# The mixer's two attentions as one pipeline of head pairs, with projections between its steps

## The chip, the cores and the metric

The kernel runs on one core of a Trainium2 chip. The metric is the device time of one execution in microseconds, as the median of three runs. The engines in the tables are TensorE (PE, with its weight loads as PEld), VectorE (DVE), ScalarE (ACT), GpSimd (POOL) and SyncE (SP, which issues the DMAs).

## The reference, cut to what matters

Two transformer blocks on 256 tokens of 1024 features. The first has two layers, each with a mixer between its feed-forward parts:

```python
(qa, ckv, iq, ik, iw, qs, ks, vs, cb, cc, ch, ga, gb, gc) = split(x @ w_in)
ckv = rms_norm(ckv, kv_g)
y_a = dsa_branch(qa, ckv, iq, ik, iw, w_uk, w_uv, rel_bias)   # 8 heads
y_b = stick_breaking_branch(qs, ks, vs)                       # 8 heads
y_c = short_conv_branch(cb, cc, ch, conv_w)
merged = (sigmoid(ga + b_gate[0]) * (y_a @ w_branch[0])
          + sigmoid(gb + b_gate[1]) * (y_b @ w_branch[1])
          + sigmoid(gc + b_gate[2]) * (y_c @ w_branch[2]))
return merged @ w_out
```

`dsa_branch` scores all earlier tokens with eight index heads (relu of dot products, weighted and added up), keeps the 64 best of each query, and then runs a softmax attention of eight heads over these, in a latent space of 128 columns that all heads share, with a bias by distance; `w_uv` takes each head's latent output to 64 columns. `stick_breaking_branch` weighs each earlier token by sigmoid(z) times the product of 1 - sigmoid(z) of the tokens between: a reverse cumulative product per row.

## The kernel before

Activations lie feature-major, [128 features, 256 tokens] a tile. Every projection is exact in float32: each operand is kept as a high and a low part, and one product is three matmuls (`mm3`, L241 to L243: high by high, high by low, low by high). Weights come in pieces of 512 KB by SP's DMA queue (`wf`), ScalarE casts the high part (`wh`, L236), VectorE subtracts it for the low part (`wl`, L237). `pair` projects two column tiles of 128 into one PSUM bank: 2 x 8 x 3 = 48 matmuls of 256 columns. PSUM has four banks with the tag `pa` (attention and transposes) and four with `pj` (projections). The pools of scratch tiles are fixed: eight of 512 columns (`a2`), four of 256 (`a1`).

The order of each engine's instructions is set by a scheduler: it takes the program as it is traced, with the tracing order as priority, and lets later instructions that are ready go ahead of earlier ones that would wait. So projections that are traced after an attention are found between its steps.

The mixer of one layer (`mixer`, L527) is traced so: values of the stick-breaking; latent and index projections; index scores, one head after the other, each in a bank of its own (L587, L588), added up on VectorE; the top-k on VectorE, 8 rounds for either half of the queries (L597, L598), and the mask `sel` (L600, L601); the attention's queries (2 pairs). Then a first pipeline of eight heads with four stages, each a head behind the one before (`skew`): `logits` (queries to latent space L626, copied by L627; bias plus mask on GpSimd L630, L631; logits L633, L634; VectorE adds the bias, L635; softmax L496 to L501 and L506), `turned` (three 128x128 transposes, L316, copied by L766), `latent` (L771, L772, copied by L649 into an `a1` tile) and `values` (L656: 64 columns of output; two heads share a bank, which is split into high and low part when the second is in). Then the queries and keys of the stick-breaking (4 pairs) and a second pipeline of eight heads with three stages: `sticks` (scores L675, L676; mask L678; two sigmoids L680, L682; the scan L687, L689), `turned`, and `broken` (L771, L772 with 64 columns of output). Then the convolution's four column tiles, 72 matmuls each, with six VectorE operations on each (L721 to L726 and the split); then 12 gate pairs, and eight output projections of the three branches (36 matmuls each) between them.

A filler runs beside all this: the second block's shifts and scales (`adaln`, L894), 4 matmuls of 32 columns a unit (L924), each unit with a weight of 512 KB (`wa`). `fill(place)` traces as many units as a table has for that visit of a place; logits and sticks have three each. `until` traces whatever is still missing when the second block needs it.

## Time and profile before

| | |
|---|---|
| median of three runs | 2645.27 us (2642.64 to 2647.34) |
| span of the profiled execution | 2638.9 us |
| TensorE busy | 2581.5 us, 98% |
| VectorE busy | 1495.0 us, 57% |
| ScalarE busy | 1176.3 us, 45% |
| stretch of the index scores and both attentions, layer 0 | 267.30 to 372.40 us |
| the same, layer 1 | 1019.90 to 1123.60 us |

Matmuls overlap in the array, so the busy time of one (0.28 us for 256 columns) is longer than the distance from its start to the start of the next; distances between starts tell what an instruction costs. "Idle before" names the engine and line that ended an idle time. The granted clock (PEclk) is a share of the full 2.4 GHz.

### The profile page before, as it was taken

How to read it: one execution, taken by the hardware profiler on the slowest of the kernel's cores; microseconds unless marked ns; L12 is line 12 of the kernel's file. 1: busy time of each engine (PE TensorE's matmuls, PEld its weight loads, DVE VectorE, ACT ScalarE, POOL GpSimd, SP SyncE). 2: the span in 40 equal slices, each digit the busy share in tenths (PEclk: the TensorE clock that was granted, in tenths of full speed). 3: DMA queues.
4: the chain of work that ended last, by engine and by line, in shares of the span. 5: the costliest groups of instructions: out<-in, count | busy, mean ns of one | idle time of the engine just before them, and what ended most of it. 6: DMA issues, size and time to landing. Idle time of an engine off the chain costs nothing.

```text
span 2638.9 us, 40347 instructions
## 1 busy us (share of the span) xinstructions
PE 2581.5 (98%) x15946; PEld 2178.1 (83%) x15946; DVE 1495.0 (57%) x3006; ACT 1176.3 (45%) x1953; POOL 43.2 (2%) x52
## 2 busy tenths in 40 slices
PE   8999999999999999999999999999999999999999
PEld 7997789969979978799699776567888776777997
DVE  5546765665456557655664757656222337555554
ACT  5444454554444444544544545444222325444443
POOL 0000100000000001000000000000000000010000
PEclk9999999999999999999999999899999999999999
DMA  7565335655556555256565542424222435432453
GB/s 256 189 216 191 133 112 181 200 204 206 189 179 208 197 173 204 90 168 205 203 223 191 184 152 80 140 102 150 104 96 96 161 106 186 121 72 64 169 192 136
DMA packets 136493, 424.19 MB, mean 161 GB/s; under 512 B 29752, under 2 KB 32480, under 8 KB 136304
## 3 DMA queue, kind: packets, MB, share of 16 engines
q1 hardware_dynamic: 136304, 421.62, 47.2%
q8 instruction: 125, 2.05, 0.3%
q14 instruction: 64, 0.52, 0.1%
HBM read 417.33 MB, written 4.24 MB: 160 GB/s over the span
## 4 chain that ended last, share of the span: by engine, by line
PE 87%; DVE 5%; DMA 4%; ACT 2%; issue 1%; SPq 0%; POOL 0%; ACTq 0%; DVEq 0%; POOLq 0%
PE pj L241 17%; PE pj L242 17%; PE pj L243 17%; PE pa L242 7%; PE pa L241 7%; PE pa L243 7%; PE pa L316 3%; PE pj L924 2%; DMA wf<-in_ffn_w_inA_dram 2%; PE pa L1392 1%; DVE wl L237 1%; DMA wa<-in_mod_wB_dram 1%; PE pj L1369 1%; DMA wf<-in_mix_A_dram 1%; PE pj L1276 1%
## 5 line engine op out<-in xcount | busy, mean ns | idle before, releaser
L237 DVE TENSOR_TENSOR wl<-wf,wh 128x1024 fp32r<-128x1024 f32 (+1 forms) x652 | 785.1, 1205 | 740.2 <-ACT wh L236 735.6
L236 ACT CAST wh<-wf 128x1024 fp32r<-128x1024 f32 (+1 forms) x652 | 670.6, 1032 | 929.9 <-PE pj L242 425.9
L241 PE MATMUL pj<-k,wh 128*128 128x256 f32 (+2 forms) x2896 | 841.7, 291 | 2.1 <-ACT k L236 2.1
L242 PE MATMUL pj<-k,wh 128*128 128x256 f32 (+2 forms) x2896 | 839.9, 290 | 0.0
L243 PE MATMUL pj<-k,wl 128*128 128x256 f32 (+2 forms) x2896 | 839.8, 290 | 0.0
L241 PEld LDWEIGHTS pj<-k,wh 128*128 128x128 f32 (+1 forms) x2896 | 555.3, 192 | 17.3 <-issue 7.0
L243 PEld LDWEIGHTS pj<-k,wl 128*128 128x128 f32 (+1 forms) x2896 | 555.0, 192 | 10.7 <-issue 3.4
L242 PEld LDWEIGHTS pj<-k,wh 128*128 128x128 f32 (+1 forms) x2896 | 555.0, 192 | 10.5 <-issue 3.2
L242 PE MATMUL pa<-wl,k 128*128 128x512 f32 x688 | 274.0, 398 | 0.0
L241 PE MATMUL pa<-wh,k 128*128 128x512 f32 x688 | 272.0, 395 | 0.0
L241 PE MATMUL pj<-wh,k 128*128 128x512 f32 (+1 forms) x616 | 247.8, 404 | 12.2 <-ACT wh L236 7.0
L242 PE MATMUL pj<-wl,k 128*128 128x512 f32 (+1 forms) x616 | 247.3, 402 | 0.0
L243 PE MATMUL pa<-wh,a 128*128 128x512 f32 x560 | 218.1, 389 | 0.0
L243 PE MATMUL pj<-wh,k 128*128 128x512 f32 (+1 forms) x496 | 198.5, 401 | 0.2 <-DVE k L237 0.2
L241 PEld LDWEIGHTS pj<-wh,k 128*128 128x128 f32 x616 | 117.4, 191 | 49.2 <-issue 8.3
L241 PEld LDWEIGHTS pa<-wh,k 128*128 128x128 f32 x688 | 128.8, 187 | 33.5 <-issue 0.8
L242 PEld LDWEIGHTS pa<-wl,k 128*128 128x128 f32 x688 | 129.2, 188 | 28.6 <-issue 1.0
L242 PEld LDWEIGHTS pj<-wl,k 128*128 128x128 f32 x616 | 117.3, 190 | 29.8 <-DVE wl L237 2.3
L236 ACT CAST k<-k 128x512 fp32r<-128x512 f32 (+2 forms) x152 | 85.7, 578 | 106.3 <-PE pa L242 39.0
L243 PEld LDWEIGHTS pa<-wh,a 128*128 128x128 f32 x560 | 105.3, 188 | 25.5 <-issue 0.4
L243 PEld LDWEIGHTS pj<-wh,k 128*128 128x128 f32 x496 | 94.9, 191 | 23.5 <-DVE jc L326 2.1
L237 DVE TENSOR_TENSOR a<-k,k 128x512 fp32r<-128x512 f32 x85 | 57.8, 687 | 50.4 <-ACT k L236 50.4
(252 smaller groups left out, 2523.4 us busy)
## 6 DMA issues: line engine op xcount, KB each, us to landing
wf<-in_ffn_w_inA_dram SPq DMA_DIRECT2D x262, 512.0 KB, 3.7
wf<-in_ffn_w_outB_dram SPq DMA_DIRECT2D x132, 512.0 KB, 3.8
wf<-in_mix_A_dram SPq DMA_DIRECT2D x108, 512.0 KB, 3.7
wa<-in_mod_wB_dram SPq DMA_DIRECT2D x96, 512.0 KB, 4.2
wf<-in_w_branchA_dram SPq DMA_DIRECT2D x32, 384.0 KB, 3.2
wf<-in_od_w_dram SPq DMA_DIRECT2D x24, 512.0 KB, 4.7
wf<-in_w_mix_outB_dram SPq DMA_DIRECT2D x16, 512.0 KB, 3.9
wf<-in_w_outB_dram SPq DMA_DIRECT2D x16, 512.0 KB, 7.9
```

The costliest lines, as they stand in the source:

```text
L236: self.nc.scalar.copy(h, x)
L237: self.nc.vector.tensor_tensor(l, x, h.bitcast(F32), ALU.subtract)
L241: mm(ps, sh, mh, start=start, stop=False)
L242: mm(ps, sh, ml, start=False, stop=False)
L243: mm(ps, sl, mh, start=False, stop=stop)
L316: self.nc.tensor.transpose(ps[:, i * P:(i + 1) * P], b, self.ident)
L924: mm(ps[32 * c:32 * c + 32, :256], self.cond[:, k], w[:, c * 256:c * 256 + 256], start=k == 0, stop=k == KT - 1)
L1276: mm(ps[:, j * T:(j + 1) * T], q["dqT"][b, h, c], k["dkT"][b, h], start=True, stop=True)
L1369: mm(ps[:, j * T:(j + 1) * T], q["qT"][hp // 4][b, hp % 4, c], k["kT"][hp // 4][b, hp % 4], start=True, stop=True)
L1392: mm(po[hp][b, c], kv[n // 2]["v"][n % 2][:, h * 64:h * 64 + 64], pT[:, n * P:(n + 1) * P], start=n == 0, stop=n == 3)
```

## The change

Index scores, stick-breaking scores and queries are computed by pairs of heads: a new function issues the matmuls of the two heads alternately, each head on its half of the array's rows and in its own bank. All six pairs of projections (queries of the attention, queries and keys of the stick-breaking) are traced ahead of the pipeline. There is one pipeline: eight units, the four head pairs of the attention and then the four of the stick-breaking, with five stages (`queries`, `weights`, `turned`, `values`, `heads`). After the second stage of each step a hook runs: a convolution tile in the steps 0 to 3, nothing in step 4, one gate pair in each step from 5 on. The latents of a pair share a bank and are copied at once (512 columns, an `a2` tile); the outputs of a pair are issued next to each other, on the two column halves of one bank. The calls of the filler at logits and sticks are gone.

```diff
-    def skew(self, units, *stages):
+    def skew(self, units, *stages, step=None):
...
             for n, stage in enumerate(stages):
                 if 0 <= t - n < len(units):
                     vals[t - n] = stage(*units[t - n], vals[t - n])
+                if n == 1 and step:
+                    step(t)
...
-        for h in range(8):
-            b = slice(64 * (h % 2), 64 * (h % 2) + 64)
-            ps = self.ps()
-            mm(ps[:, 0:P], iqT[b, h // 2, 0:P], ikT[b, 0:P], start=True, stop=True)
-            mm(ps[:, P:384], iqT[b, h // 2, P:T], ikT[b, :], start=True, stop=True)
...
+        for hp in range(4):
+            banks = self.causal_scores(iqT[:, hp], ikT)
...
-        def logits(h, _):
-            hp, i = divmod(h, 2)
-            if i == 0:
-                qls[hp] = self.a2().rearrange("p (c t) -> p c t", c=2)
-                for j in range(2):
-                    b = slice(64 * j, 64 * j + 64)
-                    ps = self.ps()
-                    mm(ps[:, :T], wuk[b, hp], qaT[b, hp], start=True, stop=True)
-                    A.mul(qls[hp][:, j], ps[:, :T], 0.125)
...
-            self.fill(f"logits{l}")
...
-        def latent(h, pT):
-            ps = self.ps()
-            self.causal_pv(ps[:, :T], [ckN[:, 0], ckN[:, 1]], pT)
-            ol = self.a1()
-            A.copy(ol, ps[:, :T])
-            return ol
-        def values(h, ol):
-            hp, i = divmod(h, 2)
-            if i == 0:
-                pos[hp] = self.ps()
-            mm(pos[hp][64 * i:64 * i + 64, :T], wuv[:, h], ol, start=True, stop=True)
-            if i == 1:
-                self.split(ys[0].h(hp), ys[0].l(hp), pos[hp][:, :T])
-        self.skew([(h,) for h in range(8)], logits, turned, latent, values)
...
-        def sticks(h, _):
-            hp, i = divmod(h, 2)
-            b = slice(64 * i, 64 * i + 64)
-            ps = self.ps()
-            mm(ps[:, 0:P], qsT[b, hp, 0:P], ksT[b, hp, 0:P], start=True, stop=True)
-            mm(ps[:, P:384], qsT[b, hp, P:T], ksT[b, hp], start=True, stop=True)
...
-            self.fill(f"sticks{l}")
...
-        def broken(h, pT):
-            hp, i = divmod(h, 2)
-            if i == 0:
-                pos[hp] = self.ps()
-            self.causal_pv(pos[hp][64 * i:64 * i + 64, :T], [vs[:, tb, h * 64:h * 64 + 64] for tb in range(NT)], pT)
-            if i == 1:
-                self.split(ys[1].h(hp), ys[1].l(hp), pos[hp][:, :T])
-        self.skew([(h,) for h in range(8)], sticks, turned, broken)
...
-        for t in range(4):
+        def conv(t):
...
+        def gate():
+            ps = self.pair(wA[15 + len(gates) // 2], xs)
...
+        def queries(kind, hp, _):
+            if kind:
+                return None
+            ql = self.a2().rearrange("p (c t) -> p c t", c=2)
+            banks = [self.ps() for _ in range(2)]
+            for j in range(2):
+                b = slice(64 * j, 64 * j + 64)
+                mm(banks[j][:, :T], wuk[b, hp], qaT[b, hp], start=True, stop=True)
+            for j in range(2):
+                A.mul(ql[:, j], banks[j][:, :T], 0.125)
+            return ql
+        def weights(kind, hp, ql):
+            if kind:
+                banks = self.causal_scores(qsT[:, hp], ksT[:, hp])
+                return [sticks(ps) for ps in banks]
+            out = []
...
+        def turned(kind, hp, ps):
+            return [self.causalT(p) for p in ps]
+        def values(kind, hp, pTs):
+            ps = self.ps()
+            if kind:
+                if hp == 0:
+                    ys[1] = Split(self, 4)
+                v = [[vs[:, tb, h * 64:h * 64 + 64] for tb in range(NT)] for h in (2 * hp, 2 * hp + 1)]
+                self.causal_pv([ps[64 * i:64 * i + 64, :T] for i in range(2)], v, pTs)
+                self.split(ys[1].h(hp), ys[1].l(hp), ps[:, :T])
+                return None
+            for i in range(2):
+                self.causal_pv([ps[:, i * T:(i + 1) * T]], [[ckN[:, 0], ckN[:, 1]]], pTs[i:i + 1])
+            ol = self.a2().rearrange("p (c t) -> p c t", c=2)
+            A.copy(ol, ps.rearrange("p (c t) -> p c t", c=2))
+            return ol
+        def heads(kind, hp, ol):
+            if kind:
+                return
+            ps = self.ps()
+            for i in range(2):
+                mm(ps[64 * i:64 * i + 64, :T], wuv[:, 2 * hp + i], ol[:, i], start=True, stop=True)
+            self.split(ys[0].h(hp), ys[0].l(hp), ps[:, :T])
+        between = {0: (conv, 0), 1: (conv, 1), 2: (conv, 2), 3: (conv, 3)}
+        def aside(t):
+            if t in between:
+                between[t][0](*between[t][1:])
+            elif t > 4:
+                gate()
+        self.skew([(kind, hp) for kind in range(2) for hp in range(4)], queries, weights, turned, values, heads, step=aside)
...
-    def causal_pv(self, ps, v, pT):
+    def causal_scores(self, q, k):
         mm = self.nc.tensor.matmul
-        mm(ps, v[0], pT[:, 0:T], start=True, stop=False)
-        mm(ps[:, P:T], v[1], pT[:, T:384], start=False, stop=True)
+        banks = [self.ps() for _ in range(2)]
+        for qs, ks, cs in ((slice(0, P), slice(0, P), slice(0, P)), (slice(P, T), slice(0, T), slice(P, 384))):
+            for i in range(2):
+                b = slice(64 * i, 64 * i + 64)
+                mm(banks[i][:, cs], q[b, qs], k[b, ks], start=True, stop=True)
+        return banks
+    def causal_pv(self, pss, vs, pTs):
+        mm = self.nc.tensor.matmul
+        for ps, v, pT in zip(pss, vs, pTs):
+            mm(ps, v[0], pT[:, 0:T], start=True, stop=False)
+        for ps, v, pT in zip(pss, vs, pTs):
+            mm(ps[:, P:T], v[1], pT[:, T:384], start=False, stop=True)
```

**TensorE, layer 0, a step of the first pipeline before.** The latent attention's transposes (L316), values (L771, L772), heads (L656) and queries (L626) stand between projections (L241 to L243); tiles with one number are one buffer.

```order
L316 MATMUL pa_2993<-ident,a_520_2947 128x128
L771 MATMUL pa_2999<-a_525_2968,k_420_2489 128x256
L316 MATMUL pa_2993<-ident,a_520_2947 128x128 x2
L772 MATMUL pa_2999<-a_525_2968,k_420_2489 128x128
L656 MATMUL pa_3004<-a_527_2973,wuk_2739 64x256
L626 MATMUL pa_3007<-k_477_2741,wuk_2737 128x256
L626 MATMUL pa_3010<-k_477_2741,wuk_2737 128x256
L656 MATMUL pa_3004<-a_536_3002,wuk_2739 64x256
L241 MATMUL pj_3308<-k_330_2158,wh_3298 128x256
L242 MATMUL pj_3308<-k_332_2160,wh_3298 128x256
```

The step's pieces are short, and the projections of later pairs follow at once.

**TensorE, layer 0, step 4 of the new pipeline**, right behind the last convolution tile. L318 are transposes, L796 and L798 the values of a pair in one bank, L694 and L695 logits.

```order
L318 MATMUL pa_3684<-ident,a_577_3394 128x128 x3
L318 MATMUL pa_3690<-ident,a_582_3412 128x128 x3
L796 MATMUL pa_3696<-a_603_3536,k_420_2489 128x256
L798 MATMUL pa_3696<-a_603_3536,k_420_2489 128x128
L796 MATMUL pa_3696<-a_605_3542,k_420_2489 128x256
L798 MATMUL pa_3696<-a_605_3542,k_420_2489 128x128
L694 MATMUL pa_3706<-k_423_2498,a_606_3544 128x128
L695 MATMUL pa_3706<-k_423_2498,a_606_3544 128x256
L694 MATMUL pa_3724<-k_423_2498,a_606_3544 128x128
L695 MATMUL pa_3724<-k_423_2498,a_606_3544 128x256
L318 MATMUL pa_3739<-ident,a_611_3558 128x128 x3
L318 MATMUL pa_3745<-ident,a_616_3576 128x128 x3
```

Before, a few pieces of one or two heads stood between projections; now the pieces of four pairs follow each other, and the values of the next pair come behind these rows.

**VectorE at the same place of the new order.** L648 to L653 are the last convolution tile's operations, L239 the subtractions for `wl` and the split, L696 the addition of the bias that frees the banks of the logits above.

```order
L239 TENSOR_TENSOR wl_4031<-wf_4028,wh_4030 128x1024
L648 TENSOR_TENSOR k_628_3675<-pj_3599,k_627_3673 128x256
L650 TENSOR_SCALAR k_629_3677<-k_628_3675,cw_3120 128x256
L651 SCALAR_TENSOR_TENSOR k_629_3677<-k_628_3675,cw_3120,k_629_3677 128x255
L652 SCALAR_TENSOR_TENSOR k_629_3677<-k_628_3675,cw_3120,k_629_3677 128x254
L239 TENSOR_TENSOR wl_4037<-wf_4034,wh_4036 128x1024
L653 TENSOR_TENSOR k_629_3677<-k_629_3677,pj_3648 128x256
L696 TENSOR_TENSOR a_636_3703<-pa_3706,a_636_3703 128x384
L239 TENSOR_TENSOR k_525_3119<-k_629_3677,k_524_3118 128x256
L498 TENSOR_REDUCE mx_3711<-a_636_3703 128x1 x2
L499 TENSOR_SCALAR mx_3711<-mx_3711 128x2
L696 TENSOR_TENSOR a_641_3721<-pa_3724,a_641_3721 128x384
```

Both additions of the bias stand behind the convolution's operations, which end on its last matmul (`pj_3648`).

**TensorE, layer 0, the stick-breaking before**: scores of one head (L675, L676), transposes, and outputs of one head (L771, L772 into 64 partitions).

```order
L316 MATMUL pa_3450<-ident,a_622_3427 128x128
L675 MATMUL pa_3456<-k_590_3171,k_589_3170 128x128
L316 MATMUL pa_3450<-ident,a_622_3427 128x128 x2
L676 MATMUL pa_3456<-k_590_3171,k_589_3170 128x256
L243 MATMUL pj_3642<-k_330_2158,wl_3627 128x256
L316 MATMUL pa_3471<-ident,a_626_3442 128x128
L241 MATMUL pj_3642<-k_330_2158,wh_3626 128x256
L316 MATMUL pa_3471<-ident,a_626_3442 128x128 x2
L771 MATMUL pa_3477<-a_628_3454,k_368_2254 64x256
L772 MATMUL pa_3477<-a_628_3454,k_368_2254 64x128
L675 MATMUL pa_3480<-k_590_3171,k_589_3170 128x128
L676 MATMUL pa_3480<-k_590_3171,k_589_3170 128x256
```

Each head's scores and outputs stand alone, with transposes or projections between them.

**TensorE, layer 0, the stick-breaking's outputs after the change**: L796 and L798 into the two halves of one bank, and the latent heads of a pair as L739.

```order
L318 MATMUL pa_4098<-ident,a_683_3903 128x128 x3
L796 MATMUL pa_4104<-a_692_3978,k_368_2254 64x256
L796 MATMUL pa_4104<-a_694_3984,k_368_2254 64x256
L798 MATMUL pa_4104<-a_692_3978,k_368_2254 64x128
L798 MATMUL pa_4104<-a_694_3984,k_368_2254 64x128
L739 MATMUL pa_4113<-a_696_3991,wuk_2739 64x256 x2
L243 MATMUL pj_4160<-k_330_2158,wh_4150 128x256
```

The two heads of a pair now stand next to each other, and there are fewer places where a projection and an attention matmul meet.

## Rows read from the trace of the kernel before

**Rows 1.** The page's busy times: us, share of the span, instructions.

```profile
PE 2581.5 (98%) x15946; PEld 2178.1 (83%) x15946; DVE 1495.0 (57%) x3006; ACT 1176.3 (45%) x1953; POOL 43.2 (2%) x52
```

**Rows 2.** Table by stretches: the index scores and attentions of both layers.

```profile
core 0: us, PE busy (x) PEld busy (x) DVE busy (x) ACT busy (x) POOL busy (x), PEclk, DMA share, GB/s
267.30:372.40 105.10, 99.92 (x661) 80.14 (x659) 76.37 (x208) 54.49 (x122) 13.00 (x16) 0.97 0.32 113
...
1019.90:1123.60 103.70, 98.72 (x664) 79.45 (x662) 76.35 (x208) 54.47 (x122) 13.04 (x16) 0.98 0.34 121
```

**Rows 3.** Timeline of PE from 293: start, us, line, tiles, shape, idle before.

```profile
295.80 0.28 PE L242 MATMUL pj<-k,wh 128*128 128x256 f32 x1
298.96 0.33 PE L316 MATMUL pa<-ident,a 128*128 128x128 f32 x1 [2.88 <-DVE a L506]
```

**Rows 4.** Table by stretches: behind that idle time, and in layer 1.

```profile
299.00:307.00 8.00, 8.00 (x29) 6.12 (x30) 4.41 (x12) 2.02 (x7) 1.50 (x2) 0.57 0.36 131
...
1052.00:1058.00 6.00, 6.00 (x27) 4.74 (x28) 3.61 (x9) 1.91 (x7) 1.64 (x2) 0.72 0.53 175
```

**Rows 5.** Waits of PE, 262 to 360, then layer 1: total, times, longest.

```profile
PE pa L316 <- DVE a L506: 4.0, 4, 2.9
PE pa L316 <- DVE a L689: 0.6, 1, 0.6
PE pa L587 <- ACT a L590: 0.3, 1, 0.3
...
PE pa L316 <- DVE a L506: 3.8, 4, 2.9
```

**Rows 6.** Timeline of PE from 362: one head's stick scores and outputs.

```profile
363.11 0.49 PE L675 MATMUL pa<-k,k 64*128 64x128 f32 x2
...
363.96 0.39 PE L243 MATMUL pj<-k,wl 128*128 128x256 f32 x1
...
364.30 0.28 PE L242 MATMUL pj<-k,wh 128*128 128x256 f32 x1
364.51 0.65 PE L771 MATMUL pa<-a,k 128*64 128x256 f32 x2
...
365.31 0.38 PE L243 MATMUL pj<-k,wl 128*128 128x256 f32 x1
365.53 0.28 PE L241 MATMUL pj<-k,wh 128*128 128x256 f32 x1
365.65 0.28 PE L242 MATMUL pj<-k,wh 128*128 128x256 f32 x1
```

**Rows 7.** Timeline of PE from 337: two heads' stick scores side by side.

```profile
339.07 0.50 PE L675 MATMUL pa<-k,k 64*128 64x128 f32 x4
...
339.93 0.38 PE L241 MATMUL pj<-k,wh 128*128 128x256 f32 x1
```

**Rows 8.** Timeline of PE from 238: the filler's column groups.

```profile
239.31 0.64 PE L924 MATMUL pj<-wa,cond 128*32 128x256 f32 x8
239.88 0.50 PE L243 MATMUL pj<-wh,k 128*128 128x512 f32 x1
```

**Rows 9.** Timeline of PE from 308.6: one latent head.

```profile
311.75 0.65 PE L656 MATMUL pa<-a,wuk 128*64 128x256 f32 x2
312.33 0.39 PE L241 MATMUL pj<-k,wh 128*128 128x256 f32 x1
```

**Rows 10.** DVE by line and shape, 385 to 485: busy, mean ns, idle before.

```profile
L237 DVE TENSOR_TENSOR wl<-wf,wh 128x768 fp32r<-128x768 f32 x16 | 15.3, 956 | 15.1 <-ACT wh L236 15.1
L753 DVE TENSOR_TENSOR k<-k,pj 128x256 f32<-128x256 f32 x18 | 7.0, 415 | 5.1 <-PE pj L243 5.1
...
L724 DVE SCALAR_TENSOR_TENSOR k<-k,cw,k 128x255 f32<-128x255 f32 x2 | 1.0, 485 | 0.1
```

**Rows 11.** Waits of PE over the whole span: the filler's weight.

```profile
PE pj L924 <- DMA wa<-in_mod_wB_dram: 4.9, 6, 1.4
```

**Rows 12.** Table by stretches: four pairs of the latent attention, columns of rows 2.

```profile
293.00:343.40 50.40, 46.30 (x289) 37.63 (x287) 30.03 (x74) 28.24 (x74) 13.00 (x16) 0.93 0.26 87
```

**Rows 13.** The same stretch, instructions on `wl` alone: PE, PEld and DVE.

```profile
293.00:343.40 50.40, 17.04 (x57) 11.30 (x57) 9.66 (x8) 0.93 0.26 87
```

More of the change, by code (lines that the diff above doesn't have):

```diff
@@ L727, in mixer @@
             self.split(ys[2].h(t), ys[2].l(t), y)
-        bg = self.t([P, 3, KT], "bg", 1)
-        self.load(bg, I["b_gateT"][l])
-        gates = []
+        def gate():
+            ps = self.pair(wA[15 + len(gates) // 2], xs)
+            for c in range(2):
+                n = len(gates)
+                if n % 4 == 0:
+                    gate.g4 = self.four()
+                A.activation(gate.g4[:, n % 4], ps[:, c * T:(c + 1) * T], AF.Sigmoid, bias=bg[:, n % 3, n // 3:n // 3 + 1])
+                gates.append(gate.g4[:, n % 4])
@@ new lines, in probabilities @@
+        def probabilities(bm):
+            p = self.a2()
+            sm = self.softmax(bm, G, 1.0, p)
+            self.scale_groups(p, G, sm)
+            return p
+        def queries(kind, hp, _):
[9 more added lines that the diff above has]
+            return ql
@@ new lines, in weights @@
+        def weights(kind, hp, ql):
[4 more added lines that the diff above has]
+            for i in range(2):
+                h = 2 * hp + i
+                bm = self.a2()[:, :384]
+                nc.gpsimd.tensor_tensor(bm[:, P:384], t5[h // 4][:, h % 4, ::-1], sel[:, P:384], ALU.add)
+                nc.gpsimd.tensor_tensor(bm[:, 0:P], t5[h // 4][:, h % 4, P - 1::-1], sel[:, 0:P], ALU.add)
+                ps = self.ps()
+                mm(ps[:, 0:P], ql[:, i, 0:P], ckT[:, 0:P], start=True, stop=True)
+                mm(ps[:, P:384], ql[:, i, P:T], ckT, start=True, stop=True)
+                V.tensor_tensor(bm, ps[:, :384], bm, ALU.add)
+                out.append(probabilities(bm))
+            return out
@@ new lines, in sticks @@
+        def sticks(ps):
+            z = self.a2()[:, :384]
+            V.tensor_tensor(z, ps[:, :384], self.masks[:, 2], ALU.add)
+            ns = self.a2()[:, :384]
+            A.activation(ns, z, AF.Sigmoid, scale=-0.125)
+            p = self.a2()
+            A.activation(p[:, :384], z, AF.Sigmoid, scale=0.125)
+            lt = z
+            for a, e in G:
+                V.memset(lt[:, e - 1:e], 1.0)
+                n = e - a
+                V.tensor_tensor_scan(lt[:, a:e - 1][:, ::-1], ns[:, e - 1:a:-1],
+                                     self.zero.broadcast_to((P, n - 1)), 1.0, ALU.mult, ALU.add)
+                V.tensor_tensor(p[:, a:e], p[:, a:e], lt[:, a:e], ALU.mult)
+            return p
@@ new lines, in heads @@
+        def heads(kind, hp, ol):
+            if kind:
+                return
+            ps = self.ps()
+            for i in range(2):
+                mm(ps[64 * i:64 * i + 64, :T], wuv[:, 2 * hp + i], ol[:, i], start=True, stop=True)
[6 more added lines that the diff above has]
+                gate()
@@ L735, in mixer @@
             while len(gates) < 3 * j + 3:
-                ps = self.pair(wA[15 + len(gates) // 2], xs)
-                for c in range(2):
-                    n = len(gates)
-                    if n % 4 == 0:
-                        g4 = self.four()
-                    A.activation(g4[:, n % 4], ps[:, c * T:(c + 1) * T], AF.Sigmoid, bias=bg[:, n % 3, n // 3:n // 3 + 1])
-                    gates.append(g4[:, n % 4])
+                gate()
             w = self.weight(I["w_branchA"][l, j], 1536)
@@ L767, in causalT @@
         return pT
[L769 removed]
+    def causal_scores(self, q, k):
         mm = self.nc.tensor.matmul
[L771 to L772 removed]
+        banks = [self.ps() for _ in range(2)]
+        for qs, ks, cs in ((slice(0, P), slice(0, P), slice(0, P)), (slice(P, T), slice(0, T), slice(P, 384))):
+            for i in range(2):
+                b = slice(64 * i, 64 * i + 64)
[7 more added lines that the diff above has]
+            mm(ps[:, P:T], v[1], pT[:, T:384], start=False, stop=True)
     def mem_kv(self, l):
```

49 lines of the change are left out of this document (11 added, 38 removed).

## The prediction

> **What bounds the kernel now.** I read the page's table of busy times first: TensorE works 2581.5 of the 2638.9 us [rows 1]. So only two things can shorten the run: less time in which TensorE is occupied, or less time in which it waits or runs at its lower clock level. The table by stretches then says where the change can act: the stretch from the first index score to the last attention output takes 105.10 us in layer 0 and 103.70 us in layer 1, with TensorE busy for 99.92 and 98.72, VectorE (DVE) for only 76.37 and 76.35, and a granted clock of 0.97 and 0.98 [rows 2]. The rest of the program holds the same instructions before and after, so the sum is made over these two stretches.
>
> Inside them the timeline shows one large hole: the last projection matmul starts at 295.80, and the next thing on TensorE starts at 298.96, after an idle 2.88 us put down to the scaling of the softmax (L506) [rows 3]. It is the first head: its logits had to wait until VectorE had finished the top-k, and nothing else was left in TensorE's queue. Behind the hole the clock is low: 0.57 over 8 us, and 0.72 over 6 us in layer 1 [rows 4], that is, a mixture of the levels 2.4 and 1.2 GHz. The view of waits has three further short waits for L506 and one for L689 [rows 5].
>
> **What goes, per layer.**
>
> a) The hole. After the change all six projection pairs (288 matmuls at the spacing of 0.12 us that 365.53 and 365.65 show [rows 6], 34.6 us) stand between the index scores and the first logits. I take the 2.9 us as gone. The cover is those six pairs; without them the hole comes back whole.
>
> b) The low clock behind it: 8.00 x 0.43 = 3.4 us in layer 0, 6.00 x 0.28 = 1.7 us in layer 1 [rows 4].
>
> c) The short waits: 4.0 - 2.9 + 0.6 = 1.7 us, and 3.8 - 2.9 + 0.6 = 1.5 us in layer 1, where the wait for L689 reads the same [rows 5]. In the new order a convolution tile (72 matmuls, 8.6 us) lies between the softmax of a pair and its transposes.
>
> d) Stick-breaking scores. One head alone takes from 363.11 to the next projection matmul at 363.96, 0.85 us [rows 6]. Two heads whose four matmuls alternate between the row halves take from 339.07 to 339.93, 0.86 us: the second head is free [rows 7]. Before, that is one adjacent pair and six single heads, 0.86 + 6 x 0.85 = 6.0; afterwards four pairs, 3.4. Saved: 2.5 us.
>
> e) Stick-breaking outputs: one head, 64 columns of the array, takes from 364.51 to 365.31, 0.80 us [rows 6]; eight of them are 6.4. Afterwards the two heads of a pair alternate between the two column halves of one bank. No row before shows two 64-column matmuls side by side. The nearest is the filler's: eight matmuls on four groups of 32 columns, all in one bank, from 239.31 to 239.88, 0.07 us each where one alone of 256 columns needs over 0.12 [rows 8]. So column groups do run together, and I take four times 0.80 and save 3.2 us. The other bound is no gain.
>
> f) Latent heads: one takes 311.75 to 312.33, 0.58 us [rows 9]; eight are 4.6, four pairs 2.3. Saved: 2.3 us, by the same argument, with the same other bound.
>
> g) Changes of the matmul's shape. Beside 0.12 us in a row, the projection matmul ahead of an attention matmul takes 0.21 (364.30 to 364.51) and the one behind it 0.22 (365.31 to 365.53) [rows 6]: 0.09 to 0.10 for each change. The order of the instructions has 65 such changes of shape in this stretch before, and 34 after; 31 x 0.09 = 2.8 us. The Trainium skill, "TensorEngine Tiling (Array Packing)", section "Key Properties", says that a change of tiling mode drains the engine; the trace agrees, with those 0.09 us, and without this sentence the term stands as it is.
>
> Per layer d) to g) are 10.8 us. With a) to c) the gain is 18.8 us in layer 0 and 16.9 in layer 1, together 35.7.
>
> **What comes, per layer.**
>
> h) Step 4 of the new pipeline has nothing between its stages. The order shows twelve rows in a row and more with transposes, values and logits of four pairs, and not one projection matmul. There, the values of pair 1 need a bank that logits of pair 3 hold until VectorE has added their bias, which stands behind the last convolution tile's operations and two weight subtractions; the heads and the first sticks wait for VectorE too. Behind the waiting matmul stand all of TensorE's later matmuls. No row before has this place. The nearest is the hole that I just removed, 2.88 us with an empty queue [rows 3], and the short waits of 0.6 us [rows 5]. I take one long and four short ones: 2.9 + 4 x 0.6 = 5.3 us. Lower bound 0 (VectorE early enough); upper bound two long ones, 2 x 2.9 + 2.4 = 8.2.
>
> i) The clock after it: mean of what followed the two holes, (3.4 + 1.7) / 2 = 2.6 us; bounds 0 and 3.4.
>
> j) Four output projections now follow each other without gates between them. Each has 36 matmuls, 4.3 us, while VectorE needs two subtractions of 0.96 us and six operations of about 0.42 us, 4.4 us [rows 10]. That is 0.1 us each, 0.4 per layer.
>
> k) The filler's units that ran at the logits and sticks are not called there any more; their TensorE time (0.07 us a matmul) is the same wherever they run. They catch up before the second block, close together, where they can wait for their 512 KB each: six such waits cost 4.9 us before, the longest 1.4 [rows 11]. I take 1.5 us in all; bounds 0 and 4.9.
>
> The latent copy (one of 512 columns for two heads), the row-half pairs of the index scores and the early loads cost nothing on the path: ScalarE is far from full, and the projections cover them.
>
> Sum: 35.7 - 2 x (5.3 + 2.6 + 0.4) - 1.5 = 17.6 us. From the profiled span of 2638.9 that gives 2621.3; the median of the runs is 6.4 us above that span, so I forecast 2645.3 - 17.6 = **2628 us**.
>
> **The rivals.**
>
> B) Step 4 does not wait at all. Then h) and i) go: 17.6 + 15.8 = 33.4 us, **2612**. For it: VectorE is busy for 73% of the stretch [rows 2]. Against it: in that step the order leaves TensorE no other work.
>
> C) The column halves do not run together, or h), i) and k) lie at their upper bounds. Without e) and f) the gain shrinks by 2 x 5.5 to 6.6 us, **2639**; with the upper bounds (2 x (2.9 + 0.8) + 3.4 more) to 6.8, the same time. The first would be the change not doing what it says; the column groups of [rows 8] speak against it.
>
> E) Banks. The pair forms need two of the four attention banks at once. The index scores already waited once for a bank, 0.3 us [rows 5]. If each of the twelve steps per layer that take two banks (index, query and stick pairs) waits so, that is 12 x 0.3 x 2 = 7.2 us, gain 10.4, **2635**. The Trainium skill's same page, section "Gotcha 1: PSUM Pressure", says that different row tiles must write to different banks and that row tiling raises the pressure on them; only that one wait of 0.3 us bears it out so far.
>
> D) Slower. VectorE becomes the bound in the four steps that hold logits and a convolution tile. Of VectorE's 30.03 us from 293 to 343.4 [rows 12], 9.7 are eight weight subtractions of 1.2 [rows 13]; the other 20.3 are four pairs, 5.1 each. A step adds three subtractions (3.7) and a convolution tile's six operations of at most 0.49 (2.9) [rows 10]: 11.7 us. TensorE has 8.6 us of projection in it; from 293 to 343.4 it had 57 projection triples, counted by their third matmuls [rows 13], 20.5 us, and 7.5 us of waits and low clock, so 22.4 us of attention, 5.6 a pair, and some 1 less after f) and g): 13.2 us. VectorE stays below as long as it loses no more than 1.5 us a step. If it loses more, TensorE waits in three further steps as at 298.96 and the clock falls each time: 3 x (2.9 + 2.6) x 2 = 33 us, which makes it 15 us slower, **2661**.
>
> **How the numbers follow.** A difference of over 0.2% (5.3 us) can be told from no change. Chances: forecast 0.50, B 0.17, E 0.11, C 0.13, D 0.09. The range runs from a little under B to a little over C, 2608 to 2641; D and the outer half of B are left out. Faster than 2640: the forecast but for its edge, B, E and half of C, 0.81; same 0.11; slower 0.08.
>
> **What would show it.** Right: no idle time ahead of the first transposes after the top-k, a granted clock of 1.00 there; two heads' outputs in about 0.8 us; a wait for VectorE in step 4, once per layer, with a lower clock behind it. The attention stretch, less the projection that is now in it, some 11 us shorter in layer 0. Wrong: waits for VectorE in each step with a convolution tile (D), pairs that take twice a head's time (C), or waits for ScalarE's bank copies (E).

## The result, and the profile after

| | before | after |
|---|---|---|
| median of the runs | 2645.38 us (2642.64 to 2647.34, 4 runs) | 2613.20 us (2612.83 to 2614.41, 4 runs) |
| span of the profiled execution | 2638.9 us | 2612.6 us |

The ratio is 0.9884, with a 95% interval of 0.9867 to 0.9901. The changed kernel is 32 us faster, by medians; between the two profiled executions it is 26.3 us. One execution of the kernel before, in the experiments, took 2933.69 us at a granted clock of 0.798 and is left out of every comparison. The forecast was 2628 in a range of 2608 to 2641: sign and range hold. The time is also that of rival B (2612), but that is luck: as will be seen, it came there by two errors of opposite sign and by the scatter of the runs.

The page of the changed kernel has TensorE as full as before, only for less time: 2555.8 us, 98% of the span [rows 1].

The attention stretch of [rows 2] now holds projections that used to come later, so it can't be compared with itself. A stretch that holds the same work in both programs goes from the last projections ahead of the index scores to the output projections that no longer differ. With its ends at the same projection matmuls (number 1600 and 2900 of all, counted from 0, and 6200 and 7200 in layer 1; I call these two stretches the mixers), the table by stretches gives, for before, with the columns of [rows 2]:

```profile
263.43:476.31 212.88, 207.70 (x1559) 187.84 (x1558) 140.82 (x303) 104.42 (x193) 13.00 (x16) 0.98 0.44 145
1028.21:1199.18 170.97, 166.28 (x1226) 147.91 (x1225) 116.14 (x260) 84.28 (x163) 13.04 (x16) 0.99 0.41 139
```

and for after:

```profile
261.46:454.80 193.34, 191.59 (x1542) 181.41 (x1541) 139.26 (x303) 102.71 (x189) 14.45 (x16) 1.00 0.49 155
1008.99:1162.26 153.27, 151.84 (x1211) 142.69 (x1210) 111.34 (x251) 82.46 (x159) 14.55 (x16) 1.00 0.44 144
```

So the mixers got 19.54 and 17.70 us shorter, 37.2 together, at a granted clock of 1.00. Of these, 3.6 us are two units of the filler a layer that stand in them only before (16 records, 1.8 us by the distances between starts: 1.23 from 283.65 and 0.56 from 286.39). The span got 26.3 shorter. The difference, 10.9 us, was lost again in the rest of the program, where the instructions are the same but for the filler's place. Both halves need an explanation: more came from the mixers than the net forecast for them, and more was given back behind them than the forecast had.

What is left of the waits in layer 0 answers to [rows 5] (total, times, longest):

```profile
PE pa L796 <- DVE a L696: 0.9, 1, 0.9
PE pa L790 <- ACT a L591: 0.4, 1, 0.4
PE pa L694 <- ACT a L780: 0.3, 1, 0.3
PE pa L790 <- DVE k L239: 0.2, 1, 0.2
```

No transposes wait for the softmax (L508, the L506 of before); the hole of [rows 3] is gone. The first and the last of these waits lie in step 4, as the timeline of TensorE shows (start, us, line, tiles, shape, count, idle before):

```profile
350.09 0.82 PE L318 MATMUL pa<-ident,a 128*128 128x128 f32 x6
351.77 0.70 PE L796 MATMUL pa<-a,k 128*128 128x256 f32 x2 [0.86 <-DVE a L696]
...
353.45 0.65 PE L739 MATMUL pa<-a,wuk 128*64 128x256 f32 x4
...
355.55 0.92 PE L790 MATMUL pa<-k,k 64*128 64x128 f32 x4 [0.19 <-DVE k L239]
...
357.31 0.92 PE L790 MATMUL pa<-k,k 64*128 64x128 f32 x4
358.15 0.39 PE L244 MATMUL pj<-k,wh 128*128 128x256 f32 x1
```

It is the place and the engine that the forecast named: the values of pair 1 wait for the bank that VectorE's addition of the bias (L696) frees. But it is 0.86 us. The heads (L739) do not wait at all, and ahead of the first sticks (L790) stand projection matmuls of the next gate, which the scheduler brought forward (from 354.03 to 355.08); the sticks wait 0.19 us. And the clock stays at full speed, 1.00 in the stretches around these waits:

```profile
350.00:354.00 4.00, 3.14 (x21) 2.19 (x19) 3.35 (x8) 1.39 (x5) 1.43 (x2) 1.00 0.42 135
354.00:358.00 4.00, 3.81 (x25) 2.94 (x23) 2.72 (x11) 2.69 (x10) 0.00 (x0) 1.00 0.02 6
```

One correction to the text ahead of the prediction: it says that logits and sticks have three calls of the filler each. The table holds three for the logits of a layer, and none for the sticks. The forecast's term k went by the units in the trace and is not touched by it.

### The profile page after: what moved, and what is told of

Same layout as the page of the kernel before. It is cut to its first block, busy times and chain, and to the rows that moved or that the text cites. A ratio compares the mean times of both kernels' runs of the same rounds, so it can differ in the third digit from the quotient of the medians.

```text
span 2612.6 us, 40313 instructions
## 1 busy us (share of the span) xinstructions
PE 2555.8 (98%) x15946; PEld 2167.1 (83%) x15946; DVE 1492.6 (57%) x3006; ACT 1174.0 (45%) x1945; POOL 48.0 (2%) x52
## 4 chain that ended last, share of the span: by engine, by line
PE 84%; DVE 7%; DMA 5%; ACT 3%; issue 1%; SPq 0%; ACTq 0%; DVEq 0%
PE pj L243 17%; PE pj L244 17%; PE pj L245 17%; PE pa L244 7%; PE pa L243 7%; PE pa L245 7%; PE pa L318 3%; PE pj L950 2%; DVE wl L239 2%; DMA wf<-in_ffn_w_inA_dram 2%; PE pa L1418 1%; ACT wh L238 1%; DMA wa<-in_mod_wB_dram 1%; PE pj L1395 1%; DMA wf<-in_mix_A_dram 1%
## 5 line engine op out<-in xcount | busy, mean ns | idle before, releaser
L239 DVE TENSOR_TENSOR wl<-wf,wh 128x1024 fp32r<-128x1024 f32 (+2 forms) x652 | 787.6, 1209 | 742.3 <-ACT wh L238 728.6
L238 ACT CAST wh<-wf 128x1024 fp32r<-128x1024 f32 (+2 forms) x652 | 670.4, 1032 | 936.6 <-PE pj L244 419.1
L243 PE MATMUL pj<-k,wh 128*128 128x256 f32 (+2 forms) x2896 | 840.7, 290 | 3.1 <-ACT k L238 3.1
L243 PEld LDWEIGHTS pj<-k,wh 128*128 128x128 f32 (+1 forms) x2896 | 553.8, 191 | 17.2 <-issue 5.7
L243 PE MATMUL pa<-wh,k 128*128 128x512 f32 x688 | 272.3, 396 | 0.0
L243 PE MATMUL pj<-wh,k 128*128 128x512 f32 (+1 forms) x616 | 248.0, 404 | 12.1 <-ACT wh L238 6.6
L243 PEld LDWEIGHTS pj<-wh,k 128*128 128x128 f32 x616 | 117.1, 190 | 49.3 <-issue 7.9
L243 PEld LDWEIGHTS pa<-wh,k 128*128 128x128 f32 x688 | 129.1, 188 | 34.0 <-issue 1.2
L239 DVE TENSOR_TENSOR a<-k,k 128x512 fp32r<-128x512 f32 x85 | 57.7, 688 | 50.8 <-ACT k L238 50.7
```

What stands on the lines that cost most here:

```text
L238: self.nc.scalar.copy(h, x)
L239: self.nc.vector.tensor_tensor(l, x, h.bitcast(F32), ALU.subtract)
L243: mm(ps, sh, mh, start=start, stop=False)
```

## The experiments

All of them are timed against the kernel before on the same chip; the ratio goes by these. A difference of 3 us between kernels of different series is near what the runs scatter.

**1. Where did the 10.9 us go? The filler's calls put back.** Three calls per layer, one behind each of the first three heads' logits; in the trace they bring two units a layer back into the mixers:

```diff
                 out.append(probabilities(bm))
+                self.fill(f"logits{l}")
```

> The changed kernel with the filler's three calls per layer put back, one behind each of the first three heads' logits of the pipeline. In the trace of the changed kernel the two mixers are 37.2 us shorter than before, but 10.9 us of that are gone again by the end: 3.6 us is the filler's own TensorE time that now stands elsewhere. Theory: the other 7 us are given back because the missing units are forced later (a wait of 2.70 us for a weight of the filler at 1257.7, of 1.94 us behind them at 1452.1, and the low clock behind these), so this kernel comes to about 2606 us (2604 to 2609). Rival: these later waits have nothing to do with the filler's place, or the units cost the mixer as much as they save; then 2612 to 2615.

Measured: 2603.11 us (2601.94 to 2608.44), ratio 0.9853 (0.9831 to 0.9874), 10 us faster than the changed kernel by medians, 8 by the ratios, and below the range of 2604 to 2609 that was expected. The two mixers are hardly longer with the units in them:

```profile
263.12:457.10 193.98, 193.11 (x1559) 181.57 (x1557) 139.33 (x303) 103.35 (x189) 13.15 (x16) 1.00 0.50 159
1010.94:1164.76 153.82, 153.33 (x1226) 142.83 (x1225) 111.38 (x251) 83.10 (x159) 13.06 (x16) 1.00 0.46 149
```

0.64 and 0.55 us more, for two units a layer inside the stretch that keep TensorE for 1.14 us: the rest fits in where it waited. Outside the mixers before has 2638.9 - 383.9 = 2255.1 us, the changed kernel 2612.6 - 346.6 = 2266.0, and this one 2601.3 - 347.8 = 2253.5. So nearly all that was lost behind the mixers was lost by moving the filler. It shows in the changed kernel's timeline as two holes, in layer 1's cross attention and in the second block's parameters:

```profile
1257.70 1.00 PE L950 MATMUL pj<-wa,cond 128*32 128x256 f32 x8 [2.70 <-DMA wa<-in_mod_wB_dram]
```

```profile
1452.12 1.69 PE L318 MATMUL pj<-ident,k 128*128 128x128 f32 x8 [1.94 <-DVE k L1021]
```

with a low clock at both,

```profile
1256.00:1262.00 6.00, 4.08 (x23) 1.61 (x24) 2.94 (x10) 2.25 (x9) 0.00 (x0) 0.72 0.74 281
1452.00:1456.00 4.00, 3.88 (x14) 3.40 (x15) 3.19 (x5) 2.76 (x6) 0.00 (x0) 0.57 0.84 232
```

and in the view of waits as 5.8 us for the filler's weight, against 2.9 in this run (all of the span; first the changed kernel, then this one; [rows 11] has 4.9):

```profile
PE pj L950 <- DMA wa<-in_mod_wB_dram: 5.8, 6, 2.7
```

```profile
PE pj L951 <- DMA wa<-in_mod_wB_dram: 2.9, 5, 1.3
```

Neither hole is in this run, nor a low clock there. Set against this run at the same projection matmuls, the changed kernel is 3.3 us ahead at number 7700 (at 1232.1 us of its span), 1.8 behind at 8000 (1320.0), 5.7 behind at 8900 (1443.3) and 9.4 behind at 9000 (1471.2): the loss falls on these two places and on the forced units between them, which run from 1417.06 to 1427.74. The theory's sum, 2606, was 3 us too cautious.

**2. The hole and its clock alone.** The kernel before, with the four projection pairs of the stick-breaking traced ahead of the first pipeline; heads stay single:

```diff
             ps = self.pair(wA[3 + u], xs)
             A.copy(qaT[:, 2 * u:2 * u + 2], ps.rearrange("p (c t) -> p c t", c=2))
+        qsT = self.four()
+        ksT = self.four()
+        for dst, u0 in ((qsT, 5), (ksT, 7)):
...
-        qsT = self.four()
-        ksT = self.four()
```

> The kernel before with one edit: the four projection pairs of the stick-breaking are traced ahead of the first pipeline, so that six pairs stand between the index scores and the first logits. Heads stay single. Theory (terms a and b of the prediction): the hole of 2.9 us and the low clock behind it go in both layers, 2.9 + 3.4 + 2.9 + 1.7 = 10.9 us, 2634 to 2635 against 2645.4. Rival: the scheduler had used these pairs to fill the gaps between single heads; taken from there, the short waits grow by what the hole gave, 2640 to 2645.

Measured: 2632.20 us (2627.36 to 2634.72), ratio 0.9952 (0.9933 to 0.9970), 11.6 us faster than before in its series (2643.79). The mixers' stretches:

```profile
262.25:468.27 206.02, 204.27 (x1559) 185.37 (x1558) 139.59 (x303) 104.37 (x193) 14.05 (x16) 1.00 0.47 150
1020.80:1186.46 165.66, 164.44 (x1226) 146.44 (x1225) 114.94 (x260) 84.30 (x163) 14.06 (x16) 1.00 0.44 143
```

6.86 and 5.31 us less than before, 12.2 together, at a clock of 1.00. Of the waits for the softmax 1.0 us is left in layer 0, where [rows 5] has 4.0:

```profile
PE pa L316 <- DVE a L506: 1.0, 2, 0.7
```

So terms a and b are right in mechanism and size (10.9 expected; the small rest is short waits that went too), and the scheduler still finds projections for the single heads. A third of the whole gain comes from the order alone, without one changed matmul.

**3. Do the column halves run together?** The changed kernel with both heads of a pair on the same 64 columns of the array:

```diff
-                self.causal_pv([ps[64 * i:64 * i + 64, :T] for i in range(2)], v, pTs)
-                self.split(ys[1].h(hp), ys[1].l(hp), ps[:, :T])
+                for i in range(2):
+                    self.causal_pv([ps[0:64, i * T:(i + 1) * T]], v[i:i + 1], pTs[i:i + 1])
+                for i in range(2):
+                    b = slice(64 * i, 64 * i + 64)
+                    self.split(ys[1].h(hp)[b], ys[1].l(hp)[b], ps[0:64, i * T:(i + 1) * T])
...
-                mm(ps[64 * i:64 * i + 64, :T], wuv[:, 2 * hp + i], ol[:, i], start=True, stop=True)
-            self.split(ys[0].h(hp), ys[0].l(hp), ps[:, :T])
+                mm(ps[0:64, i * T:(i + 1) * T], wuv[:, 2 * hp + i], ol[:, i], start=True, stop=True)
...
```

> The changed kernel with both heads of a pair on the same 64 columns of the array (stick-breaking outputs and latent heads; the second head to other columns of the bank, with one split for each head). All other work is the same, the result too. Theory (terms e and f): in the changed kernel the second head of a pair is free, here it takes its own time, some 0.65 us for a stick-breaking output and 0.43 us for a latent head, 8 pairs per layer of either kind half: 2 x 4 x 1.08 = 8.6 us slower than the changed kernel, 2620 to 2624. Rival: column halves of one bank never ran together: within 2 us of 2613.

Measured: 2623.19 us (2622.02 to 2626.69), ratio 0.9923 (0.9906 to 0.9940), 10 us slower than the changed kernel. The timeline settles it more closely than the time does. Two stick-breaking heads on two halves, in the changed kernel:

```profile
391.28 0.65 PE L796 MATMUL pa<-a,k 128*64 128x256 f32 x4
391.76 0.39 PE L798 MATMUL pa<-a,k 128*64 128x128 f32 x4
392.08 0.38 PE L243 MATMUL pj<-k,wh 128*128 128x256 f32 x1
```

and on one half:

```profile
394.80 0.65 PE L801 MATMUL pa<-a,k 128*64 128x256 f32 x2
395.29 0.38 PE L803 MATMUL pa<-a,k 128*64 128x128 f32 x2
395.50 0.59 PE L801 MATMUL pa<-a,k 128*64 128x256 f32 x2
395.94 0.38 PE L803 MATMUL pa<-a,k 128*64 128x128 f32 x2
396.25 0.39 PE L243 MATMUL pj<-k,wh 128*128 128x256 f32 x1
```

0.80 us from 391.28 to 392.08 against 1.45 from 394.80 to 396.25. The 0.80 is what one head alone takes in [rows 6]: the second head is free. Two latent heads take 0.58 us on two halves (364.15 to 364.73) and 0.96 on one:

```profile
364.15 0.65 PE L739 MATMUL pa<-a,wuk 128*64 128x256 f32 x4
364.73 0.39 PE L243 MATMUL pj<-k,wh 128*128 128x256 f32 x1
```

```profile
386.37 1.03 PE L742 MATMUL pa<-a,wuk 128*64 128x256 f32 x4
387.33 0.94 PE L795 MATMUL pa<-k,k 64*128 64x128 f32 x8
```

Four of each make 4 x (0.65 + 0.38) = 4.1 us a layer. The stretches of both layers grew by 3.0 us each (196.33 against 193.34 in layer 0), somewhat less, since in this run the two heads of the first sticks happened to run side by side, which takes 1.22 us instead of the 0.85 and 0.84 of the changed kernel (355.55 and 357.31 above). The other 4 us of the 10 lie outside the mixers, 2.5 of them ahead of the first one, where the two kernels do the same; nothing ties them to the halves. The Trainium skill, "TensorEngine Tiling (Array Packing)", section "Key Properties", says that different tiles of the array can run their weight loads and matmuls in parallel; the 0.80 against 1.45 us agree.

**4. Is step 4 dearer than its waits?** A gate pair in step 4 too:

```diff
-            elif t > 4:
+            else:
```

> The changed kernel with a gate pair (48 matmuls, 5.8 us) in step 4 too, which has no projection. Theory from the trace of the changed kernel: step 4 waits only 0.86 + 0.19 us in layer 0 and 0.93 + 0.19 in layer 1, and the clock stays at 1.00, so there are at most 2.2 us to gain: 2611 to 2613. Rival (terms h and i of the prediction, 5.3 + 2.6 us a layer): step 4 costs more than its marked waits show; then 2600 to 2606.

Measured: 2613.47 us (2611.30 to 2613.66), ratio 0.9881 (0.9863 to 0.9899): the same as the changed kernel within what can be told. The two stretches are these:

```profile
265.49:456.92 191.43, 190.54 (x1542) 181.17 (x1541) 139.33 (x303) 102.79 (x189) 14.47 (x16) 1.00 0.49 156
1010.06:1161.27 151.21, 150.80 (x1210) 142.46 (x1209) 107.97 (x243) 82.11 (x159) 14.39 (x16) 1.00 0.45 145
```

They are 1.9 and 2.1 us shorter than in the changed kernel: the marked waits and the 0.5 to 0.8 us that the first sticks' heads cost by running apart. In the profiled execution the 4 us are given back ahead of the first mixer (its stretch begins at 265.49 instead of 261.46), where both kernels do the same; among them are a wait of 1.1 us for VectorE (L574, at 263.32) and a longer time at the low clock near 50 us. So step 4 costs 2 us a layer, not 7.9; terms h and i were sized wrong, not hidden elsewhere.

**5 and 6. Rival D's point.** Idle VectorE operations of 128x256, three or nine behind each convolution tile:

```diff
             self.split(ys[2].h(t), ys[2].l(t), y)
+            for _ in range(3):
+                V.tensor_scalar(self.idle, y, 1.0, None, ALU.mult)
```

> The changed kernel with three idle VectorE operations of 128x256 (0.35 us each, 1.06 us in all) behind each convolution tile, so in each of the four steps that hold logits. Nothing else changes. Rival D put VectorE at 11.7 us against TensorE's 13.2 a step, so that 1.5 us more a step would start to cost. In the trace of the changed kernel VectorE is busy for 32.60 of the 42.71 us of these four steps, so 2.5 us a step are free. By either number 1.06 us costs nothing: 2612 to 2615. If VectorE's order already bounds these steps (its work comes late, not much), 4 x 1.06 x 2 = 8.5 us are lost and more with the clock: 2621 or above.

> The same with nine idle operations, 3.18 us a step. By rival D's point (1.5 us a step) TensorE loses 1.7 us a step, 13 us in all, and the clock falls behind the waits, 2626 to 2640. By the free time in the trace of the changed kernel (2.5 us) it loses 0.7 us a step, 5 us, 2618 to 2620. If step 4 and the long run of projections take it up, 2613 to 2615.

Measured: 2616.53 us (2612.68 to 2617.65), ratio 0.9890 (0.9874 to 0.9907), and 2616.20 us (2614.85 to 2621.77), ratio 0.9896 (0.9881 to 0.9911). Both are about 3 us above the changed kernel by medians, 1.6 and 3.2 by the ratios, and 1.5 and 1.2 us above the ranges expected for work that is taken up. The mixers of experiment 5 are as long as the changed kernel's (193.33 and 153.19 us), those of experiment 6 1.4 and 2.7 us longer. Even nine operations, 3.2 us a step and 25 us of VectorE's time in all, make no wait in the four steps with a convolution tile; in layer 0 the longest waits are these:

```profile
PE pa L799 <- DVE a L699: 1.4, 1, 1.4
PE pa L318 <- ACT a L734: 1.1, 1, 1.1
```

Both lie in step 4; two more are 0.4 us at the index scores and 0.2. So VectorE was nowhere near the bound, and both points, 1.5 and 2.5 us a step, were too low: the likely reason, which I did not test, is that the transposes that need VectorE come a whole step later. What VectorE is late shows in step 4, where no projection stands ahead of the waiting values.

**7 and 8. Better versions.** Experiment 1 and experiment 4 together; and experiment 1 with one more unit of the filler at each of the four stick-breaking pairs:

```diff
-                return [sticks(ps) for ps in banks]
+                out = [sticks(ps) for ps in banks]
+                self.fill(f"sticks{l}")
+                return out
```

> The changed kernel with the three filler calls back in the pipeline and a gate pair in step 4 too. The filler calls alone gave 2603 us; behind them the waits of step 4 are only 0.19 + 0.19 us a layer. So the gate should add nothing, 2601 to 2605. If a projection between the two single heads' scores of step 4 lets them run as a pair, up to 1.7 us more.

> The changed kernel with the filler's three calls back at the logits and one more at each of the four stick-breaking pairs, eight units more in all. Theory (a unit in this pipeline costs its 0.57 us there and saves as much where it stood, and the waits for its weight with it): the forced units ahead of the second block and their wait of 1.26 us go, 2599 to 2602. Rival: the units are then missing where they cover the holes of the cross attention and of the second block: 2604 to 2612.

Measured: 2600.72 us (2599.45 to 2604.59), ratio 0.9836 (0.9821 to 0.9851), the fastest of all and clear of the changed kernel's interval; from experiment 1 it can't be told apart by its time, though its mixers are 1.7 us shorter in each layer in the trace (192.31 and 152.17 us). The extra units, with four entries for them in the table: 2604.64 us (2603.14 to 2605.40), ratio 0.9848 (0.9833 to 0.9862), no better than without them. The rival was right there: the units are missing in another place. In layer 1's cross attention TensorE now waits 1.78 us for a softmax (L508, at 1266.63), which it does not in experiment 1, and the clock falls there, to 0.86 from 1262 to 1274.

**9 and 10. Step 4 with a late VectorE.** Sixteen idle operations behind the first product of the last convolution tile, without and with a gate pair in step 4:

```diff
             V.tensor_tensor(z, ps[:, :T], hh, ALU.mult)
+            if t == 3:
+                for _ in range(16):
+                    V.tensor_scalar(self.idle, z, 1.0, None, ALU.mult)
```

> The changed kernel with 16 idle VectorE operations of 128x256 (5.6 us) behind the first product of the last convolution tile alone; seven of them (2.5 us) stand ahead of the addition of the bias for which step 4 waits. The outputs are the same. This makes the late VectorE of the prediction's terms h and i. Theory: the mechanism is right and only its size was off, so the wait of 0.86 us grows by 2.5 us to some 3.4 us in each layer, further short waits follow, and behind a hole of that size the clock falls as it did behind the one of 2.88 us before (1.7 to 3.4 us): 2 x (2.5 + 2.5) = 10 us on 2613, 2619 to 2627. Rival: other instructions of TensorE move ahead of the waiting ones, or the idle work is taken up by VectorE's free time as in the run with nine operations a step: 2613 to 2617.

> The same with a gate pair (5.8 us of projection) in step 4. Theory: the projection is the cover that step 4 lacks; the waits of the run without it go but for some 0.5 us a layer, and the clock holds: 2612 to 2616. Rival: the bank that waits stands ahead of the projection in TensorE's queue, so the wait remains: as without the gate pair, 2619 to 2627.

Measured: 2617.95 us (2616.70 to 2619.87), ratio 0.9904 (0.9890 to 0.9918), 5 us slower than the changed kernel where I had expected 10; and 2616.14 us (2614.32 to 2620.78), ratio 0.9898 (0.9883 to 0.9913), where the gate pair was expected to take nearly all of it away; by these times the two can't be told apart. Both expectations were half right. In the first the scheduler moved projections ahead of the waiting values; the timeline:

```profile
353.66 0.55 PE L318 MATMUL pa<-ident,a 128*128 128x128 f32 x3 [1.23 <-ACT a L735]
353.97 0.36 PE L243 MATMUL pj<-k,wh 128*128 128x256 f32 x1
...
355.87 0.70 PE L800 MATMUL pa<-a,k 128*128 128x256 f32 x2 [1.07 <-DVE a L700]
```

The wait for VectorE is 1.07 us and not 3.4: five projection matmuls of the next gate came first. In the second the wait only moved on, to the first sticks, behind the gate pair:

```profile
362.36 1.30 PE L794 MATMUL pa<-k,k 64*128 64x128 f32 x8 [2.31 <-ACT a L784]
```

There it is 2.3 us in each layer, for the copies of transposed tiles on ScalarE that free the banks. They are late for two reasons, as ScalarE's timeline of layer 0 shows: the softmax ahead of them is late by VectorE (L501 ends at 359.79), and then the gate pair's own sigmoid stands in front of them, with a table load:

```profile
359.81 1.28 ACT L666 ACT_TABLE_LOAD   x1
361.83 0.86 ACT L784 COPY a<-pa 128x384 f32<-128x384 f32 x2
```

So the gate pair covers VectorE's wait and brings 2 us of ScalarE's work of its own ahead of the copies. In experiment 4 the same load stands there (at 361.47), and the first sticks wait only 0.19 us. What this kernel would do with a cover that needs no ScalarE was not tried.

## Why the prediction was right or wrong

By the terms of the sum, in layer 0, from the distances between the starts of the instructions in the stretch of 212.88 and 193.34 us:

| term | forecast | measured |
|---|---|---|
| a, c: the hole and the short waits | -4.6 | -4.7, all of it |
| b: the clock | -3.4 | 1.00 in the whole stretch, as forecast |
| d: stick scores | -2.5 | -1.8 (6.5 to 4.7) |
| e: stick outputs | -3.2 | -3.7 (6.8 to 3.1) |
| f: latent heads | -2.3 | -2.3 (4.6 to 2.3) |
| g: changes of shape, and all other TensorE time | -2.8 | -3.2 (what is left, with 1.8 taken off for the filler) |
| h: step 4 | +5.3 | +1.05 there, +0.24 at the index scores and logits |
| i: the clock behind step 4 | +2.6 | 0 |

**a, b and c** held, and experiment 2 shows them by themselves.

**d to g** held in sum, 11.0 us against 10.8, and e and f each by itself (experiment 3). Term d was 0.7 us too large: of the four pairs of sticks the first stands in step 4, where the banks come free one at a time, and its two heads ran one after the other, 0.84 us from 357.31 to 358.15 for the second, as much as a lone head before [rows 6]. That the three others also take about 1.0 us instead of the 0.86 of [rows 7] I did not follow up. The changes of shape were counted rightly: in the two traces TensorE changes the shape 65 and 34 times in layer 0's stretch. What they cost was not measured by an experiment of its own; 3.2 us is what remains after the other terms (in layer 1 too), 0.10 us for each of the 31.

**h and i** are the first step that failed. The wait was found where the order of the instructions said it would be, on the bank and behind the operation that the forecast named. Its size was taken from the nearest row, the hole of 2.88 us, and that row was the wrong neighbour. There, when TensorE ran dry at 296.08, the top-k that the forecast blamed was over (the mask was done at 293.0). The addition of the first head's bias had then waited 1.04 us for GpSimd's bias plus mask (L631) and begun at 295.17, so nearly the whole softmax was still ahead, with a weight subtraction in the midst of it; VectorE before:

```profile
296.87 1.21 DVE L237 TENSOR_TENSOR wl<-wf,wh 128x1024 fp32r<-128x1024 f32 x1
298.63 0.54 DVE L506 TENSOR_SCALAR a<-a,sm 128x128 f32<-128x128 f32 x2
```

In step 4, when TensorE ran dry at 350.91, two operations were left, one of them running; VectorE after:

```profile
350.84 0.41 DVE L653 TENSOR_TENSOR k<-k,pj 128x256 f32<-128x256 f32 x1
351.17 0.55 DVE L696 TENSOR_TENSOR a<-pa,a 128x384 f32<-128x384 f32 x1
```

And of the four short waits that the forecast added for the heads and the first sticks, 2.4 us, only 0.19 came: projections of the next gate stand there after all. Experiment 4 shows that no more than 2 us a layer is hidden there, and experiments 6 and 9 that even 3 to 6 us more of VectorE's work make the waits there only some 2.5 us long together. The clock did not fall behind this wait, so i went with it. Together this is 6.9 us a layer, 13.7 us in all, that the forecast gave away. Rival B was the better reading, but not for its reason: step 4 does wait.

**k** is the second. The filler's own time moved as forecast, at most 1.8 us a layer (1.23 + 0.56 before, 1.14 where the units run whole). The waits were bounded by 4.9 us, with 1.5 taken, from the waits for its weight alone. Measured: 10.9 - 3.6 = 7.3 us, or somewhat more, were lost beside its own time, above the upper bound. The bound left out what a forced unit does to its neighbours: it waits where something else would have run (2.70 us at 1257.70), other work queues up behind it (1.94 us at 1452.12), and the clock falls at both, 1.7 us each time ((1 - 0.72) x 6 and (1 - 0.57) x 4). Experiment 1 shows that putting three calls per layer back brings 8 to 10 us. The forecast treated the calls' removal as a detail of bookkeeping; it cost a quarter of what the pipeline had won.

The two errors: +13.7 (h, i) and -5.8 (k) on a forecast of 17.6 make 25.5 us, beside 26.3 between the profiled executions. The other 6 us of the difference of the medians come from the profiled execution of before, whose span is 6.4 us under the median while the changed kernel's is 0.6 under; the forecast had carried the 6.4 over. The 25 other executions of before in the experiments scatter by 14 us, and largely with the granted clock: 2638.31 us at 0.990 and 2652.66 us at 0.985 over the whole execution, where 0.5% of 2640 us is 13 us. What makes the clock differ from one execution to the next stays open.

**j** can't be told from nothing. **Rival C** is refuted by experiment 3 in its first half; of its second half (h, i and k at their upper bounds) only k came true. **Rival D** is refuted by experiment 6. **Rival E**: the four waits for a bank a layer, 0.9, 0.4, 0.3 and 0.2 us, are 3.6 us in both layers instead of 7.2. Only two of them, 0.4 at the index scores (0.3 before) and 0.2 at the first sticks, stand ahead of pairs on the row halves. The Trainium skill's page "TensorEngine Tiling (Array Packing)", section "Gotcha 1: PSUM Pressure", says that row tiling raises the pressure on the banks; the trace agrees, with no more than these 0.6 us a layer. The longest of the four is caused by the missing cover in step 4, since it goes when a gate stands there (experiment 4).

## What to carry to other kernels

Take the size of a new wait from what its releaser still has to do ahead of the release, operation by operation, and not from the longest wait in the old trace. When a change drops or moves background work, price the place where it will be forced in, with the waits, the queue behind it and the clock, and not only its own time; then try to keep its calls, since on a full TensorE they cost little where transfers are already in. And do the reordering that covers a hole first: here it gave a third of the gain without touching a matmul.

## What the runs showed of the hardware that I had not expected

The clock does not follow from the length of a wait alone. At the second block's parameters the changed kernel's wait of 1.94 us came with a clock of 0.57 over 4 us. In experiment 5 the wait at that place is longer, and the clock stays at 1.00:

```profile
1457.01 1.06 PE L318 MATMUL pj<-ident,k 128*128 128x128 f32 x8 [2.52 <-DVE k L1024]
```

```profile
1456.00:1460.00 4.00, 2.99 (x17) 2.63 (x18) 2.93 (x6) 2.19 (x5) 0.00 (x0) 1.00 0.58 190
```

In experiment 9 both layers have the same two waits in step 4, of 1.23 and 1.07 us. In layer 0 the granted clock stays at 1.00, in layer 1 it falls (PEclk is the third figure from the end):

```profile
353.00:357.00 4.00, 2.27 (x14) 1.99 (x15) 4.00 (x13) 0.61 (x2) 0.53 (x2) 1.00 0.33 94
```

```profile
1090.00:1094.00 4.00, 2.93 (x14) 2.46 (x13) 3.97 (x14) 0.77 (x3) 0.00 (x0) 0.71 0.36 131
```

So the price of a wait of that size is uncertain by some 1.7 us ((1 - 0.71) x 4, and half a microsecond in the next four), and a forecast should carry both.
